# Splitting weights into a high and a low part: on the compute engines, or by two DMAs issued from GpSimd

## Chip, cores and metric

The kernel runs on one core of one Trainium2 chip. The metric is device time in microseconds of one execution, lower is better; before the change it was 2781.72 us, the median of 3 runs (2781.6 to 2782.51).

## What is computed

A trunk of four pre-norm residual layers on an input of 512 tokens by 1024 features, all float32. Layers 0 and 3 mix tokens by stick-breaking attention ("sb"), layer 1 by a chunked gating MLP ("gm"), layer 2 by a Mamba-2 SSD ("ssd"); a SwiGLU feed-forward network ("ffn") follows each. Cut to what matters here:

```
for i in range(4):
    h = rmsnorm(x, mix_norm[i])
    m = [attention, gmlp, mamba2, attention][i](h)   # h @ w_in ... @ w_out
    x = x + m
    h = rmsnorm(x, ffn_norm[i])
    x = x + (silu(h @ w_gate) * (h @ w_up)) @ w_down
```

Nearly all the work is products of a 512-row activation with weight matrices that are read once each, some 236 MB in all.

## The kernel before, in words

**Three products for one.** TensorE multiplies in a reduced float32 form (`F32R`). To keep the precision, every operand is split: a high part `hi`, which is the value cast to `F32R`, and a low part `lo`, the value minus `hi`, cast too. `mm3` then issues three matmuls, hi·hi, hi·lo and lo·hi. Activations (`xh`, `xl`, and `hi`, `lo` of intermediate results) are split by ScalarE, VectorE and GpSimd as they are made; `to_hi` casts, `to_lo` subtracts.

**The weight stream.** Class `Stream` brings the weights in, in the fixed order of the stages. A *piece* is 128 partitions by 4 rows of 256 columns, 512 KB (some are smaller), and there are 469. Before the change, SyncE's queue loads a raw tile of two pieces (`raw`, 1 MB, `RAWB` = 2 buffers) with one plain DMA; then, piece by piece, `to_hi` casts it into `whi` and `to_lo` writes `wlo` = raw − whi. `whi` and `wlo` have `WB` = 3 buffers each. When TensorE has used a piece, `release` lets `issue` start the next one, so pieces are made ready while TensorE works on those ahead.

**The order is planned, not found on the chip.** Class `Order` keeps a model clock for each engine while the program is built: `A`, `V`, `G` for ScalarE, VectorE, GpSimd, `D` for the DMA. Generators such as `_split` yield the time at which a step should be done, and each instruction goes into its engine's queue when the model says that its inputs are ready. `pick` and `either` choose between engines by booked times. On the chip each engine works its queue strictly in that order; an instruction whose input is late holds up all those behind it. A DMA that GpSimd issues stands in GpSimd's own queue between its arithmetic.

**The stages.** In "ffn", `fm` takes two pieces for a pair of feature tiles; a full piece is 24 matmuls of 512 columns. In "sb", a chain of softplus-like steps (`scores`, `weigh`, `values`) runs over ScalarE, VectorE and GpSimd, and a `Filler` puts projections between; there GpSimd does `r<-s,r` (low parts of the scores) and `n<-s,a` (normalised heads) for TensorE. At the start, `setup` loads x in four DMAs (`xin`), transposes it, and makes `xh`, `xl`, the squares `sq` and their sum `acc`; `first` slips the first raw tile between the loads of x. At the end of a sublayer, `norm_in` makes `xh` on ScalarE and `xl` on VectorE from each finished tile of x.

Of the kernel before, what the change touches and what calls it, by code (L numbers as in the profile page):

```python
# [20 lines left out]
F32 = mybir.dt.float32  # L21
F32R = mybir.dt.float32r
AF = mybir.ActivationFunctionType
ALU = mybir.AluOpType
AX = mybir.AxisListType

P = 128
D = 1024
# [9 lines left out]

LAT, TO_PE, FROM_PE = 0.15, 0.27, 0.2

WB, RAWB = 3, 2

SB_ORDER = "q0 k0 v0 q1 k1 q2 v1 k2 o0 v2 q3 k3 o1 v3 o2 o3 o4".split()
O_PAIRS = ((0, 2), (2, 4), (4, 6), (6, 7), (7, 8))
# [14 lines left out]
class Task:  # L59


    def __init__(self, end=None):
        self.end, self.waiters = end, []
# [241 lines left out]
class Stream:  # L305


    def __init__(self, k):
        self.k, self.o = k, k.o
        self.raws, self.pieces = [], []  # L310
        self.next_raw = self.next_piece = 0
        self.done_raw = 0
        self.slack = 0.0

    def add(self, srcs, cuts, side=False):


        raw = {"srcs": srcs, "left": len(cuts)}
        self.raws.append(raw)
        out = []  # L320
        for c in cuts:
            p = {"raw": raw, "cut": c, "n": len(self.pieces), "task": Task(), "side": side}
            self.pieces.append(p)
            out.append(p)
        return out

    def dma(self, dst, srcs, n):

        b0 = 0
        for q in srcs:  # L330
            self.k.nc.sync.dma_start(dst[:, :, b0:b0 + q.shape[2]], q)
            b0 += q.shape[2]
        return Task(self.o.book("D", 0.00143 * n) + 2.0)

    def load(self):
        while self.next_raw < min(len(self.raws), self.done_raw + RAWB):
            r = self.raws[self.next_raw]
            self.next_raw += 1
            a, b = r["srcs"][0].shape[1], sum(q.shape[2] for q in r["srcs"])
            t = self.k.wp.tile([P, 2048], F32, tag="raw", name="raw", bufs=RAWB)  # L340
            r["ap"] = t[:, :a * b].rearrange("p (a b) -> p a b", b=b)
            r["task"] = self.dma(r["ap"], r["srcs"], a * b)

    def first(self):

        r = self.raws[0]
        self.next_raw = 1
        t = self.k.wp.tile([P, 2048], F32, tag="raw", name="raw", bufs=RAWB)
        r["ap"] = t.rearrange("p (a b) -> p a b", b=256)
        for n, p in enumerate(self.pieces[:2]):  # L350
            ks = slice(4 * n, 4 * n + 4)
            p["loaded"] = self.dma(r["ap"][:, ks, :], [q[:, ks, :] for q in r["srcs"]], 1024)
            yield

    def issue(self):
        if self.next_piece >= len(self.pieces):
            return
        p = self.pieces[self.next_piece]
        self.next_piece += 1
        self.load()  # L360
        self.o.spawn(self._split(p))

    def _split(self, p):
        nc, o, r = self.k.nc, self.o, p["raw"]
        yield p.get("loaded") or r["task"]
        a0, a1, b0, b1 = p["cut"]
        src, n, b = r["ap"][:, a0:a1, b0:b1], (a1 - a0) * (b1 - b0), b1 - b0
        hi = self.k.wp.tile([P, 1024], F32R, tag="whi", name="whi", bufs=WB)
        lo = self.k.wp.tile([P, 1024], F32R, tag="wlo", name="wlo", bufs=WB)
        if p["side"]:  # L370
            p["both"] = hi[:, :2 * n].rearrange("p (a b) -> p a b", b=2 * b)
            h, l = p["both"][:, :, :b], p["both"][:, :, b:]
        else:
            h = hi[:, :n].rearrange("p (a b) -> p a b", b=b)
            l = lo[:, :n].rearrange("p (a b) -> p a b", b=b)
        yield self.k.to_hi(h, src, n, (a1 - a0) % 2 == 0)
        yield self.k.to_lo(l, src, h, n, self.slack)
        p["h"], p["l"] = h, l
        r["left"] -= 1
        if not r["left"]:  # L380
            self.done_raw += 1
            self.load()
        o.finish(p["task"])

    def release(self, p):
# [7 lines left out]
class Trunk:  # L393
# [120 lines left out]
    def setup(self):  # L514
        nc, io, c, o = self.nc, self.io, self.const, self.o
        self.xT = [self.res.tile([P, S], F32, name=f"x{d}") for d in range(KT)]
        self.xh = [self.res.tile([P, S], F32R, name=f"xh{d}") for d in range(KT)]
        self.xl = [self.res.tile([P, S], F32R, name=f"xl{d}") for d in range(KT)]
        self.renew_norm()
        self.cols = {}  # L520
        self.ident = c.tile([P, P], F32, name="ident")
        make_identity(nc, self.ident)
        self.ones = c.tile([P, P], F32, name="ones")
        nc.gpsimd.memset(self.ones, 1.0)
        self.mhalf8 = self.tiny.tile([P, 8], F32, name="mhalf")
        nc.gpsimd.memset(self.mhalf8, -0.5)
        self.mhalf = self.mhalf8[:, :TB]
        with self.tc.tile_pool(name="xin", bufs=1, reuse_waits="tile") as pool:
            r0 = self.row_loads(pool)
            self.exp_ln()  # L530
            xv = io["x"][0].rearrange("(t p) f -> p t f", p=P)
            xtok, there, first = [], [], self.stream.first()
            for q in range(4):
                v = pool.tile([P, TB, 256], F32, name=f"xin{q}")
                nc.sync.dma_start(v, xv[:, :, q * 256:(q + 1) * 256])
                there.append(Task(o.book("D", 1.43) + 3.0))
                xtok.append(v)
                if q % 2 == 1:
                    next(first)
            for _ in range(WB):  # L540
                self.stream.issue()
            self.sb_consts(pool)
            o.until(lambda: 4.5)
            ps = self.bank()
            self.transpose(ps[:, 0:64], r0)
            self.cols[0] = self.const.tile([P, 64], F32, name="cols0")
            nc.vector.tensor_copy(self.cols[0], ps[:, 0:64])
            self.give(at=o.V(64))
            o.aside(self.more_columns())
            for q in range(4):  # L550
                for e in range(2):
                    o.until(self.both(o.due(there[q]), self.bank_cond("x")))
                    ps = self.bank("x")
                    for t in range(TB):
                        self.transpose(ps[:, t * P:(t + 1) * P], xtok[q][:, t, e * P:(e + 1) * P])
                    o.spawn(self.x_in(q * 2 + e, ps))
# [1214 lines left out]
```

## Time and profile before

| What | Value |
|---|---|
| median of 3 runs | 2781.72 us |
| profiled execution, its own time | 2782.54 us |
| its span in the trace | 2780.6 us |
| TensorE busy | 2751.9 us (99% of the span) |
| VectorE busy | 1764.4 us (63%) |
| ScalarE busy | 941.5 us (34%) |
| GpSimd busy | 522.7 us (19%) |
| granted TensorE clock | 0.999 of full speed |
| read from HBM | 236.38 MB, 86 GB/s over the span |

The profiled execution took 1.9 us more than its span, and 0.8 us more than the median of the runs. Busy times are sums over an engine; DMA-issuing instructions are not counted as busy, so a queue can be occupied by them without showing it. "DMA share" is the mean busy share of the 16 DMA engines; it counts packets that overlap, and so can go a little above 1.

### The profile page before, as it was taken

Reading aid. Unit: us, or ns where it says so; the run is one execution under the profiler, and the core shown is the slowest. Engines: PE = TensorE matmul, PEld = TensorE weight load, DVE = VectorE, ACT = ScalarE, POOL = GpSimd, SP = SyncE. Lnnn points to the kernel's source line nnn. Section 1 sums busy time; section 2 is a strip of 40 time slices with the busy share of each in tenths; the row PEclk is TensorE's granted clock in tenths of the full one; section 3 lists DMA queues with packets and bytes.
Section 4 is the critical chain, followed back from the end, with each engine's and each line's share of the span. In section 5 each row is a group of like instructions: output and inputs, shape, how many; then the busy total and the mean of one; then the engine's idle time right before and its main releaser. Section 6 shows DMA issues by size and latency. Waiting matters only on the chain.

```text
span 2780.6 us, 35816 instructions
## 1 busy us (share of the span) xinstructions
PE 2751.9 (99%) x14723; PEld 2378.6 (86%) x14723; DVE 1764.4 (63%) x2514; ACT 941.5 (34%) x1587; POOL 522.7 (19%) x397
## 2 busy tenths in 40 slices
PE   9999999999999999999999999999999999999999
PEld 8998788888988888888898898888888999788887
DVE  7787754555465655455887787754545887865453
ACT  4876410113322311112553353310113786511111
POOL 4665400002011100001311011200004656400000
PEclk9999999999999999999999999999999999999999
DMA  4111232323332232323222222222323111222322
GB/s 134 53 61 31 91 106 91 100 90 110 103 97 93 91 106 91 102 91 97 77 76 76 76 76 76 91 91 96 101 84 99 62 47 54 79 97 91 103 91 80
DMA packets 212643, 240.77 MB, mean 87 GB/s; under 512 B 6512, under 2 KB 179696, under 8 KB 212480
## 3 DMA queue, kind: packets, MB, share of 16 engines
q1 hardware_dynamic: 212224, 238.36, 27.0%
q8 instruction: 115, 1.88, 0.3%
q14 instruction: 48, 0.39, 0.1%
q0 software_dynamic: 160, 0.11, 0.0%
q10 hardware_dynamic: 96, 0.03, 0.0%
HBM read 236.38 MB, written 2.10 MB: 86 GB/s over the span
## 4 chain that ended last, share of the span: by engine, by line
PE 95%; DVE 2%; POOL 1%; issue 1%; DMA 1%; ACT 1%; SPq 0%; POOLq 0%; ACTq 0%; DVEq 0%
PE ps L458 85%; PE z L458 4%; PE c L458 3%; PE t L458 1%; DVE xl L616 1%; PE c L472 1%; PE t L472 0%; DMA ws<-in_gm_w_s 0%; DVE x L646 0%; DMA xin<-in_x 0%; POOL r L502 0%; POOL wlo L502 0%; ACT whi L479 0%; DVE sp_r L1024 0%; PE ps L472 0%
## 5 line engine op out<-in xcount | busy, mean ns | idle before, releaser
L458 PE MATMUL ps<-xh,whi 128*128 128x512 f32 x1792 | 701.9, 392 | 0.0
L458 PE MATMUL ps<-xl,whi 128*128 128x512 f32 x1792 | 698.5, 390 | 2.8 <-DVE xl L616 2.5
L458 PE MATMUL ps<-xh,wlo 128*128 128x512 f32 x1792 | 697.6, 389 | 0.0
L479 ACT CAST whi<-raw 128x1024 fp32r<-128x1024 f32 (+2 forms) x252 | 246.6, 979 | 967.2 <-PE ps L458 913.1
L500 DVE TENSOR_TENSOR wlo<-raw,whi 128x1024 fp32r<-128x1024 f32 (+2 forms) x371 | 450.4, 1214 | 119.9 <-ACT whi L479 102.5
L458 PEld LDWEIGHTS ps<-xl,whi 128*128 128x128 f32 x1792 | 336.4, 188 | 76.8 <-DVE xl L616 7.1
L481 DVE CAST whi<-raw 128x1024 fp32r<-128x1024 f32 (+1 forms) x217 | 150.2, 692 | 395.2 <-PE ps L458 394.1
L458 PEld LDWEIGHTS ps<-xh,wlo 128*128 128x128 f32 x1792 | 336.3, 188 | 70.3
L458 PEld LDWEIGHTS ps<-xh,whi 128*128 128x128 f32 x1792 | 336.4, 188 | 70.2 <-issue 1.0
L458 PE MATMUL ps<-lo,whi 128*128 128x512 f32 x960 | 373.9, 389 | 1.7 <-POOL lo L502 1.7
L458 PE MATMUL ps<-hi,whi 128*128 128x512 f32 x960 | 375.5, 391 | 0.0
L458 PE MATMUL ps<-hi,wlo 128*128 128x512 f32 x960 | 373.7, 389 | 0.0
L458 PE MATMUL ps<-whi,xh 128*128 128x256 f32 x1280 | 365.5, 286 | 0.0
L458 PE MATMUL ps<-whi,xl 128*128 128x256 f32 x1280 | 362.4, 283 | 0.4 <-DVE xl L616 0.3
L458 PE MATMUL ps<-wlo,xh 128*128 128x256 f32 x1280 | 362.1, 283 | 0.0
L502 POOL TENSOR_TENSOR wlo<-raw,whi 128x1024 fp32r<-128x1024 f32 (+1 forms) x97 | 202.6, 2089 | 301.5 <-ACT whi L479 198.7
L458 PEld LDWEIGHTS ps<-whi,xh 128*128 128x128 f32 x1280 | 245.2, 192 | 1.6 <-issue 0.2
L458 PEld LDWEIGHTS ps<-wlo,xh 128*128 128x128 f32 x1280 | 245.3, 192 | 1.1
L458 PEld LDWEIGHTS ps<-whi,xl 128*128 128x128 f32 x1280 | 245.1, 192 | 1.0 <-DVE xl L616 1.0
L502 POOL TENSOR_TENSOR acc<-acc,sq 128x512 f32<-128x512 f32 x31 | 48.5, 1565 | 1041.8 <-ACT sq L630 1041.0
L458 PEld LDWEIGHTS ps<-lo,whi 128*128 128x128 f32 x960 | 180.3, 188 | 38.8 <-POOL lo L502 2.3
L458 PEld LDWEIGHTS ps<-hi,wlo 128*128 128x128 f32 x960 | 180.2, 188 | 37.8
(227 smaller groups left out, 3386.5 us busy)
## 6 DMA issues: line engine op xcount, KB each, us to landing
raw<-in_ffn_w_gu SPq DMA_DIRECT2D x88, 1024.0 KB, 5.1
raw<-in_ffn_w_down SPq DMA_DIRECT2D x32, 1024.0 KB, 5.1
raw<-in_sb_w_qkv SPq DMA_DIRECT2D x23, 1024.0 KB, 5.1
raw<-in_gm_w_in SPq DMA_DIRECT2D x16, 1024.0 KB, 5.4
raw<-in_ssm_w_in SPq DMA_DIRECT2D x16, 1024.0 KB, 5.4
raw<-in_ffn_w_down SPq DMA_DIRECT2D x16, 768.0 KB, 4.4
raw<-in_gm_w_out SPq DMA_DIRECT2D x8, 1024.0 KB, 5.1
raw<-in_ssm_w_in SPq DMA_DIRECT2D x16, 512.0 KB, 4.9
```

The source lines that it names most:

```text
L458: self.nc.tensor.matmul(out, lhsT=lhsT, rhs=rhs, start=start, stop=stop, skip_group_check=True)
L472: self.nc.tensor.transpose(out, in_, self.ident[:in_.shape[0], :in_.shape[0]])
L479: self.nc.scalar.copy(h, src)
L481: self.nc.vector.tensor_copy(h, src)
L500: self.nc.vector.tensor_tensor(out, a, b, op=op)
L502: self.nc.gpsimd.tensor_tensor(out, a, b, op=op)
L616: nc.vector.scalar_tensor_tensor(out=self.xl[d], in0=x, scalar=gcol(d), in1=self.xh[d].bitcast(F32), op0=ALU.mult, op1=ALU.subtract)
```

## The change

The raw tile goes, and with it `load`, `first` and the two instructions of each piece on the compute engines. Instead each piece takes four steps in a row: GpSimd issues a DMA that reads the weights from HBM and casts them into `whi`; ScalarE writes −`whi` into `wlo`; GpSimd issues a second DMA that reads the same weights again and adds them into `wlo`. `whi` and `wlo` get five buffers each in place of three. The planner books 1.0 us of GpSimd for each of these DMAs and 2.5 us of latency after the transfer.

```diff
-WB, RAWB = 3, 2
+WB = 5
...
-    def dma(self, dst, srcs, n):
-
-        b0 = 0
-        for q in srcs:
-            self.k.nc.sync.dma_start(dst[:, :, b0:b0 + q.shape[2]], q)
-            b0 += q.shape[2]
-        return Task(self.o.book("D", 0.00143 * n) + 2.0)
...
+    def dma(self, dst, p, add):
+
+        a0, a1, b0, b1 = p["cut"]
+        at = 0
+        for q in p["srcs"]:
+            lo, hi = max(b0 - at, 0), min(b1 - at, q.shape[2])
+            if lo < hi:
+                d = dst[:, :, at + lo - b0:at + hi - b0]
+                if add:
+                    self.k.nc.gpsimd.dma_start(d, q[:, a0:a1, lo:hi], accum_op=ALU.add)
+                else:
+                    self.k.nc.gpsimd.dma_start(d, q[:, a0:a1, lo:hi])
+                self.o.book("G", 1.0)
+            at += q.shape[2]
+        return Task(self.o.book("D", 0.00143 * (a1 - a0) * (b1 - b0)) + 2.5)
...
     def _split(self, p):
-        nc, o, r = self.k.nc, self.o, p["raw"]
-        yield p.get("loaded") or r["task"]
+        nc, o = self.k.nc, self.o
...
-        yield self.k.to_hi(h, src, n, (a1 - a0) % 2 == 0)
-        yield self.k.to_lo(l, src, h, n, self.slack)
+        yield self.dma(h, p, False)
+        nc.scalar.mul(l, h, -1.0)
+        yield o.A(n)
+        yield self.dma(l, p, True)
         p["h"], p["l"] = h, l
-        r["left"] -= 1
-        if not r["left"]:
-            self.done_raw += 1
-            self.load()
         o.finish(p["task"])
...
-            xtok, there, first = [], [], self.stream.first()
+            xtok, there = [], []
...
-                if q % 2 == 1:
-                    next(first)
```

How the queues change is seen in GpSimd's queue at three places. The first is the start of the program, behind the constants. Before, five small loads of gains and biases (`rows`) and a sum of squares stand there:

```order
L583 DMA rows_150<-in_gm_b_in 16x128
L584 DMA rows_150<-in_gm_v_gain 16x128
L585 DMA rows_150<-in_ssm_conv_b 32x128
L586 DMA rows_150<-in_ssm_norm_gain 16x128
L587 DMA rows_149<-in_ssm_conv_w 128x128
L502 TENSOR_TENSOR acc<-acc,sq 128x512
L1484 MEMSET Q_234 64x512
```

Now the casting loads of the first five pieces stand ahead of these, and their adding loads behind the zeroing of `Q` and a sum of squares:

```order
L335 DMA whi<-in_sb_w_qkv 128x4x256 x5
L562 DMA rows_160<-in_gm_b_in 16x128
...
L566 DMA rows_159<-in_ssm_conv_w 128x128
L1463 MEMSET Q_238 64x512
...
L483 TENSOR_TENSOR acc<-acc,sq 128x512
L333 DMA wlo<-in_sb_w_qkv 128x4x256 x5
L672 TENSOR_TENSOR rstd<-ms,mhalf 128x4
```

The first product needs `whi` and `wlo` of piece 0, so an adding load in place of a subtraction on VectorE is now the last step ahead of it. The same place in ScalarE's queue, where the first −`whi` (L360) stands between the tiles of x:

```order
L593 ACTIVATE xh_90<-x,cols_157 128x512
L609 ACTIVATE sq<-x_78 128x512
L360 ACTIVATE wlo<-whi 128x1024
L593 ACTIVATE xh_91<-x,cols_157 128x512
L360 ACTIVATE wlo<-whi 128x1024 x2
L609 ACTIVATE sq<-x_79 128x512
```

The negation of piece 0 has moved in behind `xh_90` and a square, and `xh_91` behind the negation. The second place is in the first attention stage, in GpSimd's queue. Before, it holds arithmetic alone:

```order
L502 TENSOR_TENSOR n<-s,a 128x512
L502 TENSOR_TENSOR wlo<-raw,whi 128x1024
L1517 TENSOR_TENSOR a<-a,mhalf 128x8
L502 TENSOR_TENSOR r<-s,r 128x512
L502 TENSOR_TENSOR n<-s,a 128x512
L502 TENSOR_TENSOR wlo<-raw,whi 128x1024
L502 TENSOR_TENSOR r<-s,r 128x512
```

Now each piece has two DMAs between the same kinds of steps:

```order
L483 TENSOR_TENSOR r<-s,r 128x512
L335 DMA whi<-in_sb_w_qkv 128x4x256
L483 TENSOR_TENSOR r<-s,r 128x512
L333 DMA wlo<-in_sb_w_qkv 128x4x256
L1496 TENSOR_TENSOR a<-a,mhalf 128x8
L335 DMA whi<-in_sb_w_o 128x2x256
L483 TENSOR_TENSOR n<-s,a 128x512
```

An `L333` waits for ScalarE's negation, and `a`, `n` and `r` stand behind it. The third place is the end of the first attention stage and the start of the first "ffn":

```order
L483 TENSOR_TENSOR lo<-of,hi 128x512
L335 DMA whi<-in_ffn_w_gu 128x4x256
L333 DMA wlo<-in_ffn_w_gu 128x4x256
L335 DMA whi<-in_ffn_w_gu 128x4x256
L333 DMA wlo<-in_ffn_w_gu 128x4x256
L483 TENSOR_TENSOR acc<-acc,sq 128x512 x2
L335 DMA whi<-in_ffn_w_gu 128x4x256
```

Through the "ffn" stages one casting and one adding load alternate. Counted over the program, two pieces are mostly between their two loads: the casting load of piece k+1 is ahead of the adding load of piece k. In all, 485 casting and 485 adding loads are issued (a piece of two sources takes two of each).

## Rows read from the trace of the kernel before

**Rows 1.** Page: span, and busy time of each engine with its share.

```profile
span 2780.6 us, 35816 instructions
PE 2751.9 (99%) x14723; PEld 2378.6 (86%) x14723; DVE 1764.4 (63%) x2514; ACT 941.5 (34%) x1587; POOL 522.7 (19%) x397
```

**Rows 2.** Waits of TensorE: total us, times, longest us.

```profile
PE t L458 <- DVE v L1537: 5.9, 4, 2.1
PE ps L472 <- DMA rows<-in_ffn_norm: 5.5, 1, 5.5
PE ps L458 <- DVE xl L616: 2.8, 5, 1.1
PE c L458 <- POOL xde L502: 2.0, 1, 2.0
PE ps L458 <- POOL lo L502: 1.7, 2, 0.9
PE z L458 <- POOL r L502: 1.6, 2, 0.8
```

**Rows 3.** Windows: first "sb", first "ffn", "gm", "ssd"; last columns clock, DMA share, GB/s.

```profile
29.00:314.00 285.00, 278.65 (x1931) 258.98 (x1929) 228.75 (x344) 196.74 (x381) 170.15 (x114) 0.99 0.18 57
314.00:664.00 350.00, 350.00 (x1546) 289.54 (x1547) 186.95 (x232) 56.31 (x71) 14.24 (x9) 1.00 0.30 97
664.00:960.00 296.00, 294.64 (x1739) 261.95 (x1738) 169.39 (x222) 90.23 (x180) 31.27 (x19) 1.00 0.32 100
1363.00:1748.00 385.00, 381.86 (x2235) 337.42 (x2233) 309.25 (x551) 170.28 (x269) 60.86 (x78) 1.00 0.25 74
```

**Rows 4.** Page, groups of instructions that write `whi` and `wlo` by compute engines.

```profile
L479 ACT CAST whi<-raw 128x1024 fp32r<-128x1024 f32 (+2 forms) x252 | 246.6, 979 | 967.2 <-PE ps L458 913.1
L500 DVE TENSOR_TENSOR wlo<-raw,whi 128x1024 fp32r<-128x1024 f32 (+2 forms) x371 | 450.4, 1214 | 119.9 <-ACT whi L479 102.5
L481 DVE CAST whi<-raw 128x1024 fp32r<-128x1024 f32 (+1 forms) x217 | 150.2, 692 | 395.2 <-PE ps L458 394.1
L502 POOL TENSOR_TENSOR wlo<-raw,whi 128x1024 fp32r<-128x1024 f32 (+1 forms) x97 | 202.6, 2089 | 301.5 <-ACT whi L479 198.7
```

**Rows 5.** Groups by shape, whole run: one full piece on ScalarE.

```profile
L479 ACT CAST whi<-raw 128x1024 fp32r<-128x1024 f32 x194 | 203.9, 1051 | 812.1 <-PE ps L458 772.2 <-issue 35.2 <-POOL a L1517 3.4
```

**Rows 6.** Windows of 2 us at the start; last two columns DMA share, GB/s.

```profile
4.00:6.00 2.00, 0.47 (x2) 0.38 (x3) 0.09 (x1) 0.00 (x0) 1.56 (x4) 1.00 1.05 354
12.00:14.00 2.00, 2.00 (x11) 2.00 (x11) 2.00 (x4) 2.00 (x5) 1.28 (x1) 1.00 1.09 349
```

**Rows 7.** DMA issues: count, KB each, median us from issue to landing.

```profile
raw<-in_sb_w_o SPq DMA_DIRECT2D x4, 512.0 KB, 3.7
...
rows<-in_ssm_conv_w POOLq DMA_DIRECT2D x1, 64.0 KB, 5.9
```

**Rows 8.** Tile `rows`: ns of each DMA issue on GpSimd, min/median/max.

```profile
L583 POOL DMA_DIRECT2D rows<-in_gm_b_in x1: 714/714/714, 2.8 to 2.8; - x1
L584 POOL DMA_DIRECT2D rows<-in_gm_v_gain x1: 490/490/490, 3.5 to 3.5; - x1
...
L587 POOL DMA_DIRECT2D rows<-in_ssm_conv_w x1: 576/576/576, 5.0 to 5.0; - x1
```

**Rows 9.** Timeline of the start: start us, us, engine, line, instruction.

```profile
2.89 0.23 DVE L1451 CAST maskr<-tmp 128x128 fp32r<-128x128 f32 x1 [0.30 <-POOL tmp L1449]
...
13.54 0.71 ACT L614 ACTIVATE xh<-x,cols 128x512 fp32r<-128x512 f32 x1
...
13.62 0.56 PE L458 MATMUL ps<-whi,xh 128*128 128x256 f32 x1
...
14.12 0.65 ACT L630 ACTIVATE sq<-x 128x512 f32<-128x512 f32 x1
```

**Rows 10.** Groups by shape in the first "sb" stage: low parts of weights on GpSimd.

```profile
L502 POOL TENSOR_TENSOR wlo<-raw,whi 128x1024 fp32r<-128x1024 f32 x19 | 47.4, 2493 | 21.8 <-DVE whi L481 15.0 <-ACT whi L479 6.7
...
L502 POOL TENSOR_TENSOR wlo<-raw,whi 128x512 fp32r<-128x512 f32 x15 | 20.6, 1371 | 14.3 <-PE t L458 6.1 <-DVE whi L481 5.9 <-ACT whi L479 2.3
```

More of the change, by code (lines that the diff above doesn't have):

```diff
@@ L309, in __init__ @@
         self.k, self.o = k, k.o
-        self.raws, self.pieces = [], []
-        self.next_raw = self.next_piece = 0
-        self.done_raw = 0
+        self.pieces, self.next_piece = [], 0
         self.slack = 0.0
     def add(self, srcs, cuts, side=False):
-        raw = {"srcs": srcs, "left": len(cuts)}
-        self.raws.append(raw)
         out = []
         for c in cuts:
-            p = {"raw": raw, "cut": c, "n": len(self.pieces), "task": Task(), "side": side}
+            p = {"srcs": srcs, "cut": c, "task": Task(), "side": side}
             self.pieces.append(p)
@@ L325, in add @@
         return out
-    def dma(self, dst, srcs, n):
-        b0 = 0
-        for q in srcs:
-            self.k.nc.sync.dma_start(dst[:, :, b0:b0 + q.shape[2]], q)
-            b0 += q.shape[2]
-        return Task(self.o.book("D", 0.00143 * n) + 2.0)
[L335 to L353, printed above, removed]
+    def dma(self, dst, p, add):
[12 more added lines that the diff above has]
+        return Task(self.o.book("D", 0.00143 * (a1 - a0) * (b1 - b0)) + 2.5)
     def issue(self):
@@ L359, in issue @@
         self.next_piece += 1
-        self.load()
         self.o.spawn(self._split(p))
     def _split(self, p):
-        nc, o, r = self.k.nc, self.o, p["raw"]
-        yield p.get("loaded") or r["task"]
+        nc, o = self.k.nc, self.o
         a0, a1, b0, b1 = p["cut"]
-        src, n, b = r["ap"][:, a0:a1, b0:b1], (a1 - a0) * (b1 - b0), b1 - b0
+        n, b = (a1 - a0) * (b1 - b0), b1 - b0
         hi = self.k.wp.tile([P, 1024], F32R, tag="whi", name="whi", bufs=WB)
@@ L375, in _split @@
             l = lo[:, :n].rearrange("p (a b) -> p a b", b=b)
-        yield self.k.to_hi(h, src, n, (a1 - a0) % 2 == 0)
-        yield self.k.to_lo(l, src, h, n, self.slack)
+        yield self.dma(h, p, False)
+        nc.scalar.mul(l, h, -1.0)
+        yield o.A(n)
+        yield self.dma(l, p, True)
         p["h"], p["l"] = h, l
-        r["left"] -= 1
-        if not r["left"]:
-            self.done_raw += 1
-            self.load()
         o.finish(p["task"])
```

## The prediction, made before the changed kernel ran

> **What bounds the kernel now.** I read the busy times first: TensorE works 2751.9 of 2780.6 us, VectorE 1764.4, the others less [rows 1]. So TensorE's work is the time, and no change to the other engines can win more than the 28.7 us in which it stands still. The waits of TensorE say where these lie: 5.5 us are the load ahead of the first transpose, and the five largest that VectorE or GpSimd ended add up to 5.9 + 2.8 + 2.0 + 1.7 + 1.6 = 14.0 us [rows 2]. The windows by stage say the same by place: TensorE is busy for 350.00 of 350 us in "ffn" and for 278.65 of 285 in "sb" [rows 3]. No wait on the weight stream is among the rows: weights are always there in time, which the change could spoil but not improve. That makes the question whether the new stream is still fast enough everywhere, and what it does to the queues that it now stands in.
>
> **What goes.** The four groups that split the weights: 246.6 us on ScalarE, 450.4 + 150.2 on VectorE, 202.6 on GpSimd [rows 4]. VectorE is relieved of 600.6 us, a third of its work, but it bounds no stage as a whole. What TensorE could get back is a part of the 14.0 us; I take 4, since the waits sit at single steps (the last xl of a sublayer, v in "sb") which the planner's order sets as much as load does. Bounds: 0 and 14.0.
>
> **ScalarE's new work.** A negation reads and writes as many elements as the cast of a full piece, 1.05 us [rows 5]. 469 of them are at most 493 us, where the 252 casts took 246.6; in "ffn" ScalarE was busy for 56.31 of 350 us, in "sb" for 196.74 of 285 [rows 3]. As a sum it fits. As a place in the queue it is taken up below.
>
> **Is the DMA fast enough?** At the start of the program the queues are full, and plain loads then move 349 to 354 GB/s at a DMA share of 1.05 to 1.09 [rows 6]: 350 GB/s is what this traffic gets at most, 1.50 us for 512 KB. An "ffn" stage reads 97 GB/s for 350 us [rows 3], 34.0 MB or 64.8 pieces, 5.40 us each. The casting load moves the same bytes as a plain one; I price it at 1.50 us. No adding load is in the trace. Below, it costs no less than a plain load, 1.50 us. Above, I take three whole transfers one after the other (read HBM, read SBUF, write SBUF), 4.50 us. I choose 3.00, a second read at the speed of the first. A piece then takes 4.50 of 5.40 us, 83% of what the DMA can do, and "gm" at 100 GB/s 86%; "ssd" (74) and "sb" (57) have more room [rows 3]. So in the dense stages the stream stays hidden by TensorE's work, at a cost of 0. The cover is gone when an adding load takes more than 5.40 − 1.50 = 3.90 us, 2.6 times a plain one.
>
> The Trainium skill, in "Collectives: The Full Stack", section "The bandwidth ceiling: the fold count and why AG ≠ RS ≠ AR", says that an add in the DMA engines costs no cycles of its own but needs two source reads on one ring, and so runs at half the rate of a copy. By it the sum would be that of the 3.00 us; no row here shows it.
>
> **Latency.** A piece is issued when the one five before it has been used, so it has some 4 × 5.40 = 21.6 us. A 512 KB load on SyncE's quiet queue lands 3.7 us after issue, a small one from GpSimd in the full queues of the start after 5.9 [rows 7]. Twice 5.9, 1.05 for the negation and 1.5 for the second read make 14.4 us. That fits, and since the casting load of piece k+1 stands ahead of the adding load of piece k in GpSimd's queue, the two latencies of neighbours overlap. Cost 0 in "ffn" and "gm".
>
> **GpSimd's queue.** A DMA issue took 490 ns for 16 partition rows and 576 for 128 [rows 8], 0.77 ns for each row more. A piece is 512 rows: 576 + 384 × 0.77 = 0.87 us. In proportion to the rows it would be 4 × 576 = 2.30 us, the upper bound; 0.49 is the lower. I take 0.87, the slope that the two rows show. 970 issues are then 844 us beside the 522.7 − 202.6 = 320 us that remain: GpSimd is under half occupied.
>
> One issue took 714 ns in place of about 490 [rows 8]. It began at 2.8, and a cast on VectorE ran from 2.89 for 0.23 us [rows 9]: about the excess. The Trainium skill, in "SBUF — State Buffer", section "SBUF: two separate sides", says that GpSimd can't write descriptors while VectorE runs a two-port copy or cast. By it, each issue could lose up to one such VectorE instruction; the 217 casts of weights, which were most of that kind, are gone [rows 4]. I add nothing.
>
> **Where it does cost: the start.** The first product began at 13.62 us [rows 9]. Now it needs the adding load of piece 0. ScalarE reaches the negation behind xh_90 and a square: the cast to xh that began at 13.54 took 0.71 and a square 0.65 [rows 9], so 14.9, and 1.05 for the negation: 16.0. Against that, one copy of x has left ScalarE ahead of it, some 0.6: 15.4. From there 3.7 us to land [rows 7] and 1.5 for the second read give 20.6, and the first product is 7 us late. Bounds: 4 (if the negation is done at 13.9 and the load takes 3.7) and 10 (5.9 in place of 3.7, and 2 more for an add at its upper price). TensorE has nothing else to do there, so all of it counts: **+7**.
>
> **Where it does cost: the in-order queues in "sb".** The planner expects a casting load to be done 1.46 + 2.5 us after issue, plus 0.15. If it lands after some 5 us, midway between 3.7 and 5.9 [rows 7], the negation holds ScalarE for 0.9 us, and the adding load holds GpSimd by as much. Behind them are the exponentials, r and n on which TensorE's chain waits. There are 40 pieces in a "sb" stage, 36 us of lateness. ScalarE idles 31% and GpSimd 40% of the stage [rows 3], GpSimd more now that 47.4 + 20.6 us of wlo are gone [rows 10], and TensorE has filler. I let one part in six through: 6 us a stage, **+12** for the two; bounds 0 and 72. "ssd" has 54 pieces but ScalarE idles 56% [rows 3]: **+3**, bounds 0 and 15. At the seven changes of sublayer a negation can stand ahead of the last xh, 0.7 us each: **+5**, bounds 0 and 10.
>
> **Sum.** 2780.6 + 1.9 outside the span = 2782.5 for the profiled execution. + 7 + 12 + 3 + 5 − 4 = 2805.5; that execution was 0.8 over the median, so 2805 us, 0.8% slower.
>
> **Rivals.**
> *The DMA becomes the bound.* If an adding load costs 4.50 us, a piece takes 6.0. An "ffn" stage: 64.8 × 6.0 = 389 us, 39 more, 156 for four; "gm" (296 us at 100 GB/s, 56.5 pieces): 339, 43 more; "ssd" (54.3 pieces, 326 us) still fits in 385. With the 23 us of the sum: 3004 us. For it: 83% is near, and casts and adds are unseen here. Against it: the second read alone doesn't reach it. It decides from 2.6 times a plain load.
> *GpSimd's issuing becomes the bound.* At 2.30 us an issue, 40 pieces take 184 us in "sb", and 170.15 − 68.0 = 102 us of arithmetic remain [rows 3, 10]: 286 of 285 us, no slack. Each adding load is then 2.9 us later than I price, and by the same one part in six 40 × 2.9 × 2 / 6 = 39 us come on top for both stages: 2844 us. In "ffn" 4.6 us still fits into 5.40. Against it: eight times the rows added only 0.09 us.
> *It is faster.* VectorE, freed of a third of its work, ends the waits of TensorE sooner: all 14.0 us come back, the start costs only 4 and the queues nothing: 2772 us. It decides where the relief is more than what the start loses. Against it: this needs all bounds at their good ends.
> *No difference*: start 6, relief 4, queues 2: 2786 us, inside 0.2%.
>
> **How the numbers follow.** A measurement of this kernel can tell about 0.2%, 5.6 us, from no change. My forecast, TensorE-bound with queue losses, 2787 to 2850: 0.60. DMA-bound: 0.20, at 2850 to 3300. GpSimd-bound: 0.07. No difference: 0.09. Faster: 0.04. So slower 0.87, same 0.09, faster 0.04. The range leaves out the faster case and part of no difference below, and the dearer half of the DMA case above: 2782 to 3080. Within the forecast alone it is 2787 to 2850.
>
> **What would show it.** Right: TensorE's busy time stays near 2752 us; the first product starts near 20.6; in "ffn" windows TensorE stays full at a DMA share near 0.8 to 0.9; adding loads land some 1.5 us after casting ones; new waits on r, n and xl in "sb". Wrong: TensorE waiting for wlo by DMA in "ffn" (the DMA bound), GpSimd issues of 2 us or more, or a first product at 14 us. An adding load above 3.9 us of DMA time would break the forecast.

## The result, and the profile after

The changed kernel took 2888.39 us (median of 4 runs, 2875.44 to 2895.76) against 2781.76: a ratio of 1.037, 95% interval 1.0358 to 1.0382. The forecast, 2805 us, had the sign; the loss is 107 us where it had 23. The time lies outside the 2787 to 2850 us of the forecast, and inside the 2850 to 3300 that the prediction gave to its rival "the DMA becomes the bound".

The page, with span and busy times, answers to [rows 1]:

```profile
span 2884.8 us, 36776 instructions
PE 2790.7 (97%) x14723; PEld 2402.1 (83%) x14723; DVE 1139.0 (39%) x1977; ACT 1135.7 (39%) x1772; POOL 1259.5 (44%) x1246
```

The span grew by 104.2 us, and TensorE's line splits this. It stands still for 2884.8 − 2790.7 = 94.1 us, 65.4 more than before; and the same 14723 matmuls are busy for 38.8 us longer. The mean granted clock fell from 0.999 to 0.985, and 1.4% of 2790 us, 39 us, is the second part. VectorE lost 625 us of work and TensorE got nothing for it.

TensorE's waits, which answer to [rows 2]:

```profile
PE ps L439 <- DVE acc L481: 16.4, 6, 7.1
PE ps L439 <- DMA wlo<-in_sb_w_qkv: 14.7, 3, 11.3
PE ps L439 <- DMA wlo<-in_gm_w_in: 8.6, 5, 3.2
...
PE t L439 <- ACT r L460: 4.4, 4, 1.6
```

The wait for `acc`, the sum of squares at a change of sublayer, is new. So is each wait on the weight stream; there was none before. Almost none of them lies inside an "ffn", as the windows show (columns as in [rows 3]). The first is the inside of an "ffn", the others are the change from "ffn" to "gm", 5 us each:

```profile
450.00:550.00 100.00, 100.00 (x443) 82.80 (x442) 15.99 (x25) 20.25 (x20) 37.38 (x37) 1.00 1.08 195
685.00:690.00 5.00, 3.91 (x17) 2.94 (x17) 0.00 (x0) 1.34 (x2) 0.00 (x0) 1.00 1.15 214
690.00:695.00 5.00, 3.71 (x18) 3.71 (x19) 2.37 (x4) 2.97 (x6) 4.08 (x4) 0.66 1.00 205
695.00:700.00 5.00, 1.76 (x12) 1.56 (x12) 2.20 (x4) 1.20 (x3) 2.72 (x3) 0.83 1.30 249
700.00:705.00 5.00, 4.14 (x20) 3.85 (x19) 1.35 (x2) 2.57 (x4) 1.30 (x1) 0.50 0.79 165
705.00:710.00 5.00, 5.00 (x30) 5.00 (x30) 1.81 (x4) 1.95 (x2) 4.03 (x5) 0.64 1.03 150
710.00:715.00 5.00, 5.00 (x39) 4.52 (x39) 1.63 (x6) 2.30 (x7) 1.76 (x4) 1.00 0.75 152
```

In the "ffn" TensorE is full, as forecast, though the DMA share is at 1.08; over the insides of the four "ffn" stages it stands still for 0.7 us of 1275. The inside of "gm" is not free of waits, which the forecast had at 0. The first line is of the kernel before, the second of the changed one; most of the 8.8 us are waits for `wlo`:

```profile
690.00:945.00 255.00, 255.00 (x1477) 226.04 (x1476) 144.57 (x186) 71.66 (x144) 21.22 (x10) 1.00 0.31 97
```

```profile
720.00:975.00 255.00, 246.20 (x1434) 217.51 (x1434) 69.69 (x119) 82.04 (x154) 83.48 (x81) 0.99 0.92 169
```

At the change from "ffn" to "gm" TensorE is short of work in four windows in a row. After the first of them the clock column reads 0.66, 0.83 and 0.50, which is the lower of the clock's two levels (1.2 of 2.4 GHz). It still averages 0.64 in a window in which TensorE was busy throughout: a wait is paid for twice.

What made the wait is in ScalarE's timeline at the same place:

```profile
680.02 1.06 ACT L360 ACTIVATE wlo<-whi 128x1024 fp32r<-128x1024 f32 x1 [0.59 <-DMA whi<-in_gm_w_in]
688.66 1.06 ACT L360 ACTIVATE wlo<-whi 128x1024 fp32r<-128x1024 f32 x1 [7.58 <-DMA whi<-in_gm_w_in]
689.62 0.70 ACT L593 ACTIVATE xh<-x,cols 128x512 fp32r<-128x512 f32 x1
690.23 0.61 ACT L609 ACTIVATE sq<-x 128x512 f32<-128x512 f32 x1
...
700.92 1.06 ACT L360 ACTIVATE wlo<-whi 128x1024 fp32r<-128x1024 f32 x1 [4.72 <-DMA whi<-in_gm_w_in]
701.88 0.71 ACT L593 ACTIVATE xh<-x,cols 128x512 fp32r<-128x512 f32 x1
```

The tile of x that this `xh` reads was finished by VectorE at 682.3, but `xh` ran at 689.6: the negation ahead of it in the queue waited 7.58 us for its casting load. The last `xh` stood behind another such wait of 4.72 us. The planner had put these negations there because it expected a casting load after 1.46 + 2.5 us.

GpSimd's queue has a part in it, too. Each adding load waits there for ScalarE's negation, and the next casting load stands behind it:

```profile
679.73 1.27 POOL L333 DMA_DIRECT2D wlo<-in_ffn_w_down  x1 [6.46 <-ACT wlo L360]
680.50 1.29 POOL L335 DMA_DIRECT2D whi<-in_gm_w_in  x1
```

GpSimd stood still for 6.46 us before the adding load, and only then issued the casting load for which the negation at 688.66 waited. So a late load delays the issue of the next one as well.

Between the matmuls that start the sums of squares, one early in each sublayer, the change adds, in order: "sb" 9.3 us, "ffn" 18.3, "gm" 19.7, "ffn" 10.5, "ssd" 7.7, "ffn" 14.6, "sb" 9.3, "ffn" 9.5, and 5.2 ahead of the first. The mark lies inside each sublayer, so a stretch holds the change into the next one.

### The profile page after: what moved, and what is told of

It is laid out like the page before. It is cut to its first block, busy times and chain, and to the rows that moved or that the text cites. A ratio compares the mean times of both kernels' runs of the same rounds, so it can differ in the third digit from the quotient of the medians.

```text
span 2884.8 us, 36776 instructions
## 1 busy us (share of the span) xinstructions
PE 2790.7 (97%) x14723; PEld 2402.1 (83%) x14723; DVE 1139.0 (39%) x1977; ACT 1135.7 (39%) x1772; POOL 1259.5 (44%) x1246
## 3 DMA queue, kind: packets, MB, share of 16 engines
q0 software_dynamic: 482624, 461.80, 88.6%
## 4 chain that ended last, share of the span: by engine, by line
PE 59%; issue 16%; POOL 10%; DMA 9%; ACT 3%; DVE 2%; POOLq 0%; ACTq 0%; DVEq 0%
PE ps L439 53%; POOL wlo L333 4%; POOL whi L335 3%; DMA whi<-in_sb_w_qkv 3%; PE z L439 3%; PE c L439 2%; DMA whi<-in_ssm_w_in 1%; DMA whi<-in_ffn_w_gu 1%; DMA whi<-in_gm_w_in 1%; ACT wlo L360 1%; PE t L439 1%; DMA whi<-in_sb_w_o 1%; POOL a L1496 1%; POOL r L483 1%; POOL m L483 0%
## 5 line engine op out<-in xcount | busy, mean ns | idle before, releaser
L360 ACT ACTIVATE wlo<-whi 128x1024 fp32r<-128x1024 f32 (+2 forms) x468 | 471.9, 1009 | 1406.9 <-DMA whi<-in_ffn_w_gu 452.5
L439 PE MATMUL ps<-wlo,xh 128*128 128x256 f32 x1280 | 368.6, 288 | 22.5 <-DMA wlo<-in_sb_w_qkv 14.7
L439 PE MATMUL ps<-whi,xh 128*128 128x256 f32 x1280 | 371.4, 290 | 0.0
L333 POOL DMA_DIRECT2D wlo<-in_ffn_w_gu x176 | 230.3, 1308 | 250.2 <-ACT wlo L360 207.9
L625 DVE TENSOR_TENSOR x<-x,ps 128x512 f32<-128x512 f32 x200 | 135.0, 683 | 466.0 <-PE ps L439 465.6
L335 POOL DMA_DIRECT2D whi<-in_ffn_w_gu x176 | 162.5, 930 | 326.1 <-PE ps L439 326.1
L439 PEld LDWEIGHTS ps<-wlo,xh 128*128 128x128 f32 x1280 | 251.3, 196 | 25.3 <-DMA wlo<-in_sb_w_qkv 15.4
L439 PEld LDWEIGHTS ps<-whi,xh 128*128 128x128 f32 x1280 | 251.4, 196 | 2.0 <-issue 0.4
L439 PEld LDWEIGHTS ps<-whi,xl 128*128 128x128 f32 x1280 | 251.2, 196 | 0.0
L439 PEld LDWEIGHTS ps<-hi,whi 128*128 128x128 f32 x960 | 181.0, 188 | 40.4 <-ACT hi L460 4.0
```

Of the source, the lines that this page charges most:

```text
L333: self.k.nc.gpsimd.dma_start(d, q[:, a0:a1, lo:hi], accum_op=ALU.add)
L335: self.k.nc.gpsimd.dma_start(d, q[:, a0:a1, lo:hi])
L360: nc.scalar.mul(l, h, -1.0)
L439: self.nc.tensor.matmul(out, lhsT=lhsT, rhs=rhs, start=start, stop=stop, skip_group_check=True)
L625: nc.vector.tensor_tensor(self.xT[d], self.xT[d], ps, op=ALU.add)
```

## Two theories

**A, order.** The planner's times for the loads are too early, so steps that wait for a load stand in in-order queues ahead of the chain of x, which TensorE needs at each change of sublayer. **B, bandwidth.** The adding loads cost so much DMA time that the stream is behind at such places, whatever the order. All times below are medians of 4 runs; those of the kernel before in the same sessions were 2784 to 2786 us.

## Later places for both loads; a load that doesn't add; the casting half alone; the negation on GpSimd

**Later places.** The only edit:

```diff
-        return Task(self.o.book("D", 0.00143 * (a1 - a0) * (b1 - b0)) + 2.5)
+        return Task(self.o.book("D", 0.00143 * (a1 - a0) * (b1 - b0)) + 6.0)
```

> The planner is told that each of the two loads lands 6.0 us after its transfer in place of 2.5; nothing else is changed. Theory A (order): in the changed kernel the negations and adding loads stand in the queues of ScalarE and GpSimd before their casting load has landed (5.4 us and more after issue, where the planner expected 4), so the squares, xh and acc behind them are late at each change of sublayer, and TensorE waits and then runs at a lower clock. Then later places take most of the 65 us of added waits and of the 39 us of longer matmuls away: 2815 to 2850 us, ScalarE's waits on casting loads fall from over 1100 us to under a half. Theory B (bandwidth): an adding load costs so much DMA time that the loads are behind whatever the order is: 2870 to 2900 us.

Measured: 2814.16 us, ratio 1.0108 (1.0091 to 1.0125). The same loads in other places cost 74 us less. TensorE's busy time came down to 2760.5 us by itself, and the clock up to 0.993. ScalarE's waits on casting loads fell from 1173 us to 776, less than I expected. The total is not what counts: the waits of negations with an `xh` or a square right behind them fell from 80 us to 0 (counted further below). B as stated is out.

**A second load that doesn't add.**

```diff
-                    self.k.nc.gpsimd.dma_start(d, q[:, a0:a1, lo:hi], accum_op=ALU.add)
+                    self.k.nc.gpsimd.dma_start(d, q[:, a0:a1, lo:hi])
```

> The second load of each piece casts the weights into the low part and does not add, so the low parts hold the weights themselves; order, count and issue places are those of the changed kernel. Theory B (bandwidth): the second load then costs as little as the first, the DMA share in the dense stages falls from 1.07 to about 0.6, and the loads are no longer late: 2800 to 2835 us. Theory A (order): the casting loads land a little sooner, since less stands ahead of them in the ring, but negations still block ScalarE: 2850 to 2885 us.

This run leaves out the add, so `wlo` holds the weights and the output is not the kernel's; it is a probe and not a version. Measured: 2798.84 us, ratio 1.0051 (1.0036 to 1.0066): 1 us below what B had said, and 51 below the range of A, though the order is that of the changed kernel. So the add is part of the cause as well. The DMA issues of the changed kernel (count, KB each, median us from issue to landing, as in [rows 7]):

```profile
whi<-in_ffn_w_gu POOLq DMA_DIRECT2D x176, 512.0 KB, 5.4
wlo<-in_ffn_w_gu POOLq DMA_DIRECT2D x176, 512.0 KB, 7.1
...
whi<-in_gm_w_in POOLq DMA_DIRECT2D x32, 512.0 KB, 8.2
```

and of the one without the add:

```profile
whi<-in_ffn_w_gu POOLq DMA_DIRECT2D x176, 512.0 KB, 4.1
wlo<-in_ffn_w_gu POOLq DMA_DIRECT2D x176, 512.0 KB, 4.9
...
whi<-in_gm_w_in POOLq DMA_DIRECT2D x32, 512.0 KB, 4.6
```

Casting loads stand behind adding loads on the same queue. Without the adds they land after 4.1 to 4.6 us, near the 4.0 that the planner expects; with them after 5.4 to 8.2. That fits one reading of both runs: what counts is landing time against planned place, and either side of it can be mended. The issue on GpSimd fell as well, by tile `wlo` (min/median/max ns, as in [rows 8]); for the changed kernel and for the one without the add:

```profile
L333 POOL DMA_DIRECT2D wlo<-in_ffn_w_gu x176: 1267/1288/1860, 309.9 to 2799.2; - x176
```

```profile
L333 POOL DMA_DIRECT2D wlo<-in_ffn_w_gu x176: 740/747/796, 298.7 to 2710.7; - x176
```

So this run takes away DMA time and 0.54 us of GpSimd's time per load together; it doesn't tell the two apart.

**The casting half alone.** The edit of `_split`, with `plain` a load by SyncE:

```diff
-        yield self.dma(h, p, False)
-        nc.scalar.mul(l, h, -1.0)
-        yield o.A(n)
-        yield self.dma(l, p, True)
+        t = self.k.wp.tile([P, 1024], F32, tag="raw", name="raw", bufs=2)
+        r = t[:, :n].rearrange("p (a b) -> p a b", b=b)
+        yield [self.dma(h, p, False), self.plain(r, p)]
+        yield self.k.to_lo(l, r, h, n, self.slack)
...
```

> The casting load is kept; the negation and the adding load go. The raw weights come by a plain load of SyncE into a buffer of one piece, and the low part is raw minus high on VectorE or GpSimd as before the change; four buffers for the parts, for space. Theory A (order): ScalarE is never blocked, but the subtraction waits for a casting load that lands later than planned, now in the queues of VectorE and GpSimd: 2790 to 2840 us. Theory B (bandwidth): two loads without add, DMA share 0.6: 2785 to 2800 us. If the casting load alone were at fault, it would stay above 2850 us.

Measured: 2824.77 us, ratio 1.0151 (1.013 to 1.0172). Casting by DMA alone, without negation or add, already costs 40 us; TensorE's largest wait is now for `xl` (15.8 us), a VectorE step like the subtractions that wait there for a casting load. Without any add about, the casting loads of "ffn" still landed late, so the adds are not the only thing that delays them:

```profile
whi<-in_ffn_w_gu POOLq DMA_DIRECT2D x176, 512.0 KB, 5.2
```

That fits A. The run's four buffers in place of five are a second difference, so the 40 us are not the casting load's price alone.

**DMA time of each kind.** The page's queue lines (packets, MB, share of 16 engines' span) for the changed kernel, the one without the add, and the casting half:

```profile
q0 software_dynamic: 482624, 461.80, 88.6%
```

```profile
q0 software_dynamic: 482624, 461.80, 72.4%
```

```profile
q0 software_dynamic: 241392, 230.96, 35.1%
q1 hardware_dynamic: 252560, 238.37, 28.4%
```

By span, 72.4% of 2794.6 us is 2023 us for twice the weights, 1012 for once. The casting half gives 35.1% of 2819.7, 990 us, for 230.96 MB by casting loads, 4.29 us per MB. Its plain queue took 801 us for 238.37 MB, which are the same weights and some 7 MB of other loads, 3.36 us per MB: a casting load takes 1.28 times a plain one. The changed kernel's 88.6% of 2884.8 is 2556. If its casting loads take the 1012 us of the run without the add, 1544 are left for the adding loads, 6.69 us per MB: 1.53 times a casting and 1.99 times a plain load.

**The negation on GpSimd.**

```diff
-        nc.scalar.mul(l, h, -1.0)
-        yield o.A(n)
+        nc.gpsimd.tensor_scalar(out=l, in0=h, scalar1=-1.0, scalar2=None, op0=ALU.mult)
+        yield o.book("G", 0.00125 * n + 0.15)
```

> The negation moves from ScalarE to GpSimd, ahead of the adding load that waits for it there in any case. Theory A, in the form that ScalarE's blocked queue is what holds xh and the squares: ScalarE no longer waits for loads, 2815 to 2850 us. In the form that GpSimd's blocked queue (acc, r and n behind an adding load) matters as much: 2860 to 2890 us. Theory B (bandwidth): no gain, and GpSimd has 469 more steps: 2880 to 2920 us.

Measured: 3568.66 us, ratio 1.2813 (1.2791 to 1.2834). No theory had this. GpSimd also issues the loads, and all steps of a piece now stand in its one queue:

```profile
473.67 2.77 POOL L360 TENSOR_SCALAR wlo<-whi 128x1024 fp32r<-128x1024 f32 x1 [2.13 <-DMA whi<-in_ffn_w_gu]
476.40 0.80 POOL L335 DMA_DIRECT2D whi<-in_ffn_w_gu  x1
477.19 1.33 POOL L333 DMA_DIRECT2D wlo<-in_ffn_w_gu  x1
480.59 2.77 POOL L360 TENSOR_SCALAR wlo<-whi 128x1024 fp32r<-128x1024 f32 x1 [2.07 <-DMA whi<-in_ffn_w_gu]
```

The negation takes 2.77 us here, where ScalarE took 1.06. With two issues and a wait of 2.1 us for the casting load a piece takes 6.9 us of the queue, and TensorE wants one every 5.40. The run thus changes the price of the negation along with its place. The dense window:

```profile
450.00:550.00 100.00, 84.98 (x341) 66.04 (x340) 20.94 (x30) 3.79 (x6) 68.13 (x42) 0.95 0.82 146
```

146 GB/s in place of 195, at a DMA share of 0.82 where 1.08 had been reached: the issuing queue is what is short, not the DMA.

## The start; still later places; both gains together

**Small loads by SyncE.** The five loads of `more_columns` move from `nc.gpsimd.dma_start` to `nc.sync.dma_start`; nothing else.

> The changed kernel with the planner's 2.5 us, but the five small loads of gains and biases are issued by SyncE, so that they no longer stand between the casting and the adding loads of the first pieces and hold GpSimd. If the start costs what the trace of the changed kernel shows (first adding load at 18.3 us, TensorE waits 11.3 us for it), the first adding load is issued at 15.5 to 16.5, the wait falls by 2 to 3 us, and the time by 2 to 5, within what the runs scatter: 2875 to 2890 us. A theory that the start is the main loss would expect 2850 or less.

Measured: 2879.13 us, ratio 1.0337 (1.0322 to 1.0353); TensorE's longest wait at the start fell from 11.3 us to 9.3, and the time by 9 us, less than the 20 us over which the changed kernel's runs scatter. The expectation for a start that is the main loss, 2850 us or less, did not come, but the run takes away only 2 us of the wait. Clearer is the run below with only the casting load later: it gains 78 us although its wait at the start is 15.3 us.

**Later places, and the old start.** Beside 6.0 us for both loads and the small loads by SyncE, the first two pieces are made in the old way:

```diff
+        if "raw" in p:
+            yield p["loaded"]
+            yield self.k.to_hi(h, p["raw"], n)
+            yield self.k.to_lo(l, p["raw"], h, n)
+        else:
+            yield self.dma(h, p, False)
...
```

> Loads planned 6.0 us late as in the first run, and at the start the first two pieces are made as before the change: raw by SyncE between the loads of x, cast and subtraction on the compute engines; the small loads of gains go by SyncE. Theory A (order) with the start as the largest rest: TensorE's wait of 13.9 us falls below 3 and the clock stays up, 2797 to 2804 us. If the rest of the 30 us lies in the dense stages (bandwidth), 2808 to 2815.

Measured: 2803.54 us, ratio 1.0065 (1.005 to 1.0081): 10.6 us less than with the later places alone. That is what the start costs there, and more than the 7 us I had for it.

**Still later.** The constant is 9.0.

> The planner is told 9.0 us in place of 6.0. Theory A (order): the loads land before their places in the queue nearly everywhere, but the two latencies now fill 21 of the 21.6 us that five buffers give, so that pieces are planned just in time: 2805 to 2830 us, TensorE waiting for the planned places of wlo rather than for ScalarE. If landing late were still the loss at 6.0, it would gain another 10 us or more: below 2804.

Measured: 2861.68 us, ratio 1.0274 (1.0257 to 1.0291). Worse than both theories allowed, and than 6.0 by 47 us. Waits for `acc` are back (20.2 us in 5, against 4.8 in 5 at 6.0), and for the weights of "gm" (10.5 us). None of it is the loss of the changed kernel: no negation with an `xh` or a square right behind it waited for its load here. I had said that two such latencies nearly fill what five buffers give; whether that is the cause, and why `acc` is late, was not taken apart.

**Later places and no add.**

> Both edits together: planned 6.0 us late, and the second load casts without adding, so that the low parts hold the weights. If order and the add's DMA time are two ways into one loss (loads later than their places), the two gains of 74 and 90 us don't add up: 2790 to 2800 us, what is left being the start. If they were separate losses, the sum would lie at or below the time of the kernel before the change: 2775 to 2785 us.

Measured: 2802.84 us, ratio 1.0064 (1.0049 to 1.0079). The gains of 74 and 90 us don't add up: a little over 2800 us, as said for two ways into one loss. The upper bound of the expected range was missed by 3 us. Where no load adds, later places gain nothing (2798.84 us without them): the early place cost only where the loads landed late. Of the waits that are left the largest is for `acc`, 15.0 us, 14.2 of them at the start.

## Which of the two places, and which engine

> Only the casting load is planned 6.0 us late, the adding load stays at 2.5. The negation of a piece now stands later in ScalarE's queue, while TensorE's use of the piece is planned as before. Theory A, with the negations ahead of xh and the squares as the step that costs: most of the 74 us that 6.0 for both gave, 2815 to 2835 us. If it is the adding load's place (products planned before wlo has landed) that costs: above 2860.

> Only the adding load is planned 6.0 us late, the casting load stays at 2.5. Negations stand where the changed kernel has them. Theory A with the negations as the step that costs: 2860 to 2890 us, ScalarE's waits on casting loads stay above 1000 us. If the products planned before wlo has landed cost: 2815 to 2835.

The edits are `+ (2.5 if add else 6.0)` and `+ (6.0 if add else 2.5)`. Measured: 2810.21 us, ratio 1.0096 (1.008 to 1.0112), with only the casting load planned later; 2884.42, ratio 1.0355 (1.0337 to 1.0374), with only the adding load. This is the clearest pair: the gain comes with the casting load's planned landing, none with the adding load's, which sets the place of the products. ScalarE's timeline with only the casting load later, at the change from "ffn" to "gm":

```profile
667.51 1.06 ACT L360 ACTIVATE wlo<-whi 128x1024 fp32r<-128x1024 f32 x1 [3.52 <-DMA whi<-in_gm_w_in]
674.18 0.72 ACT L593 ACTIVATE xh<-x,cols 128x512 fp32r<-128x512 f32 x1 [5.61 <-DVE x L625]
674.81 0.62 ACT L609 ACTIVATE sq<-x 128x512 f32<-128x512 f32 x1
675.33 1.04 ACT L360 ACTIVATE wlo<-whi 128x1024 fp32r<-128x1024 f32 x1
676.31 0.72 ACT L593 ACTIVATE xh<-x,cols 128x512 fp32r<-128x512 f32 x1
...
682.13 1.06 ACT L360 ACTIVATE wlo<-whi 128x1024 fp32r<-128x1024 f32 x1
689.57 1.06 ACT L360 ACTIVATE wlo<-whi 128x1024 fp32r<-128x1024 f32 x1 [6.38 <-DMA whi<-in_gm_w_in]
```

The first `xh` now waits for x and nothing else, and the negations between the tiles of x find their loads landed. The one that still waits 6.38 us has no tile of x behind it.

Counted over ScalarE's whole timeline, this is what changed. A negation that waited for its casting load, with an `xh` or a square right behind it that had no wait of its own, stands in 19 places of the changed kernel, 80.3 us in all; with only the adding load later in 20, 85.0 us; with only the casting load later, and with both later, in none. The run without the add, whose order is that of the changed kernel, has 4 of them with 4.5 us, although its waits on casting loads still add up to 1048 us.

One rival is not separated from it. The adding load is issued behind the negation, so a later negation also moves the adding load in GpSimd's queue, and GpSimd waits less for negations. The first line is of the changed kernel, the second with only the casting load later:

```profile
POOL wlo L333 <- ACT wlo L360: 663.3, 285, 10.0
```

```profile
POOL wlo L333 <- ACT wlo L360: 348.6, 227, 6.6
```

No run here frees one of the two queues and leaves the other as it was.

**The negation on VectorE.** `nc.vector.tensor_scalar(out=l, in0=h, scalar1=-1.0, ...)`, booked there, in the places of the changed kernel:

> The changed kernel with the planner's 2.5 us, but the negation is done by VectorE. Theory A in the form that any queue with the chain of x in it pays for a step that waits on a load (VectorE adds the residual and makes xl): no gain, 2865 to 2900 us. If it were ScalarE's load (its squares and xh behind 1 us negations, waits or not) that costs: 2820 to 2850, since VectorE is idle 60% and does the negation in about 0.7 us.

Measured: 3116.36 us, ratio 1.1195 (1.1177 to 1.1212). The sign is that of A, the size far beyond it. VectorE waits for casting loads now:

```profile
DVE wlo L360 <- DMA whi<-in_ffn_w_gu: 559.7, 105, 9.8
DVE wlo L360 <- DMA whi<-in_ffn_w_down: 398.7, 72, 9.7
```

VectorE empties PSUM in every stage (gate, up, residual), so the loss is no longer at changes of sublayer alone: TensorE is idle for 235 us. VectorE's waits on casting loads add up to 1304 us, ScalarE's in the changed kernel to 1173: of the two, ScalarE was the less harmful one to block.

**A middle place.** The kernel with the old start, at 4.5 in place of 6.0:

> The kernel with the old start (first two pieces raw, small loads by SyncE), planned 4.5 us late in place of 6.0 for both loads. Landing took 5.0 us for casting and about 7 for adding loads in the dense stages, so 1.46 + 4.5 is near the first and short of the second. If the time is flat between too early and too late: 2796 to 2810 us. If 6.0 is still too early for the changes of sublayer: above 2815. A version faster than the kernel before would have to come below 2782, which the remaining waits (some 42 us of idle TensorE against 28.7) speak against.

Measured: 2801.86 us, ratio 1.0064 (1.0048 to 1.008), the best that adds on the way; between 4.5 and 6.0 the time is flat. TensorE is idle for 40 us of the span, against 28.7 before the change, and busy for 2758.4 against 2751.9. No version here beats the kernel before.

## Why the prediction was off, step by step

- **What bounds the kernel, and the dense stages**: right for "ffn", where TensorE is 100.00 us busy in 100, but not for "gm", where the term was 0 and 8.8 us were lost in 255. VectorE's 625 us of relief brought nothing, not even the 4 us that I took back.
- **The rival "the DMA becomes the bound"**: the time fell into its range, but not for its reason. Its sign was to be TensorE waiting for `wlo` in "ffn", and the insides of those stages stand still for 0.7 us in all.
- **The price of the loads**: the add was right (3.00 us, twice a plain load; measured 1.99 times). That agrees with the rule of the Trainium skill in "Collectives: The Full Stack", section "The bandwidth ceiling: the fold count and why AG ≠ RS ≠ AR", by which an add runs at half the rate of a copy; against a casting load it is 1.53 times. The casting load was mis-sized: not a plain load's time but 1.28 times it. With 1.28 + 1.99 in place of 1 + 2 a piece takes an estimated 4.9 of 5.40 us, 91%, and I went wrong in what followed from it: I asked only whether the DMA keeps up, and priced the answer at 0. The pieces of "ffn" still came in time, but each load landed later.
- **The step that failed is the term "the in-order queues"**, +12 for "sb", +3 for "ssd" and +5 for the changes of sublayer, and above all the last. I had seven negations ahead of the last `xh`, each 0.7 us late. Measured were 19 negations that held an `xh` or a square, with 80.3 us of wait, 4.2 us each. The landing I had from two rows, 3.7 and 5.9 us [rows 7], as 5 us (their midpoint is 4.8); casting loads landed after 5.4 us in "ffn" and 8.2 in "gm", behind adding loads in one queue, and single waits were 7.58 and 4.72 us. The place was named rightly; the number of places and the lateness were far too small. With the casting load planned later those waits are gone, and 78 of the 107 us with them. In "sb", 9.3 us a stage were measured for the 6 I had, the change to "ffn" included.
- **What was left out of that term**: the loop between the two queues. I counted that the casting load of piece k+1 stands ahead of the adding load of piece k, which helps, and not that the casting load after it stands behind that adding load, which waits for ScalarE. GpSimd spent 663 us in such waits.
- **What was missing is the clock.** I counted waits at their own length. In 5 us windows, busy time times what the clock was short of 1 adds up to 31.6 us in the changed kernel, 1.8 before, and 11.8 with only the casting load later; it is a rough measure of the 38.8 us of longer matmuls. The runs that lost most of their waits, the one without the add and those with the casting load 4.5 or 6.0 us late, have a mean clock of 0.993 to 0.996.
- **The start**: TensorE resumed at 24.3 where I had 20.6. ScalarE's negation was done at 15.24, close to my 15.4, but GpSimd reached the adding load only at 18.34, after loads of gains that by the profile themselves waited for casting loads (timeline; last bracket is the wait):

```profile
11.79 0.49 POOL L565 DMA_DIRECT2D rows<-in_ssm_norm_gain  x1 [3.54 <-DMA whi<-in_sb_w_qkv]
...
14.16 1.08 ACT L360 ACTIVATE wlo<-whi 128x1024 fp32r<-128x1024 f32 x1
14.51 0.57 POOL L566 DMA_DIRECT2D rows<-in_ssm_conv_w  x1 [2.23 <-DMA whi<-in_sb_w_qkv]
...
18.34 6.50 POOL L333 DMA_DIRECT2D wlo<-in_sb_w_qkv  x5
...
24.34 0.58 PE L439 MATMUL ps<-wlo,xh 128*128 128x256 f32 x1 [11.27 <-DMA wlo<-in_sb_w_qkv]
```

  I had followed ScalarE's queue to the negation, and not GpSimd's to the load. My upper bound of 10 us was also added up wrongly: by its own parts (2.2 for the later landing, 1.5 to 2 for the dearer add) it is 10.7 to 11.2. Against the 13.62 of before, 24.34 is 10.7 us late.
- **GpSimd's issue**: 0.87 us was priced for each; a casting load took 0.76, an adding one 1.29 (medians of the "ffn" loads). GpSimd did not become the bound: it was busy for 1259.5 us, 44% of the span. Contrary to the note under the table of the kernel before, the profile counts GpSimd's DMA issues as busy: these 1259.5 us hold 975 of them.

What stays open: how the gain without the add divides between DMA time and GpSimd's issue time, how the gain of the later casting load divides between ScalarE's queue and GpSimd's, and why a constant of 9.0 brings waits for `acc` back.

## What to carry to other kernels

Where each engine works its queue in order, ask of every step that waits on a DMA not only whether the data come often enough but what stands behind that step, and price the lateness at the places where the cover is thin: changes of stage, and the start. Here a DMA that casts landed later than a plain one of the same size (5.2 against 3.8 us in the casting half), and one behind adding loads later still; if a planner sets the order, its latencies have to be those of the trace, since one such constant was worth about 70% of the loss. Where the engine that issues the loads also waits for one of them, look for the loads that stand behind that wait. Count a TensorE wait with the slow clock that follows it.

## What the hardware showed that I had not expected

A load that casts took 1.28 times the DMA time of a plain load, byte for byte, both measured in one run (990 us for 230.96 MB and 801 us for 238.37 MB), and one that adds 1.99 times. An adding load held GpSimd for 1.29 us where the casting one of the same shape, at the same place, took 0.75. After a window in which TensorE was busy for 3.91 of 5 us, the granted clock averaged 0.66, then 0.83 and 0.50 in the next three, and 0.64 in the one after, in which TensorE was busy throughout. GpSimd negated a full piece in 2.77 us where ScalarE took 1.06.
